# A float32 encoder on one core: seven block products for every round of the channel mixer's second product but the last, and GpSimd for most low parts of the weights

## The chip, the core and the metric

The kernel runs on one core of a Trainium2 chip. The metric is the device time of one execution in microseconds. The engines that matter are TensorE (PE, matmuls; PEld is its weight loads), VectorE (DVE), ScalarE (ACT), GpSimd (POOL) and SyncE (SP, which issues the loads). Each runs its own queue in order; semaphores tie the queues together.

## The reference

The program is a trunk of two residual layers over 256 positions and 2048 channels, in float32.

```python
for i in range(DEPTH):                     # DEPTH = 2
    j = i // 2
    h = rms_norm(x, ...)                   # layer 0: convolution and pooling; layer 1: Fourier mix
    ...
    x = x + mixed @ w_out
    h = rms_norm(x, mlp_norm[i])
    x = x + jnp.square(jax.nn.relu(h @ mlp_w1[i])) @ mlp_w2[i]     # 2048 -> 8192 -> 2048
    g = jax.nn.sigmoid(rms_norm(x, ple_norm[i]) @ ple_w_gate[i])
    x = x + g * (p[i] @ ple_w_proj[i])
return rms_norm(x, final_norm)
```

## The kernel before

**Matmuls in three passes.** A float32 matrix is split into two parts that TensorE takes in its faster float32 form: a high part (hi), and a low part (lo) that is the float minus the high part. A product is hi·hi + hi·lo + lo·hi, three matmuls. Weights are streamed from HBM once, so their splitting runs all the time: `Weights.load` has SP fetch a tile `raw` of 128x2048 floats (1 MB; four buffers), and `Weights.divide` makes `hl` from it (four buffers): ScalarE writes hi (line 112), and another engine writes lo = raw − hi (line 117). Which one is the argument `lo`. Before, that is GpSimd for 28 of the tiles in layer 0's token mixer and VectorE for all others. `next()` hands out one `hl` tile, and calls for the splitting of the three behind it and the loading of two more.

**The channel mixer** (`mlp`) works through the 8192 hidden channels in 16 groups `q` of 512. `w1(q)` makes one group's hidden values in transposed form, with four tiles `hl`: 16 matmuls of 512 columns and 16 of 256 for each; afterwards ScalarE and VectorE evict them (lines 608, 609), apply relu, the norm's scale `rows` and the square, and split them into `h`. Two groups make a round `f`; `w2(f, n)` multiplies them by the 512 output columns number `n` (48 matmuls for each of two tiles).

**Seven block products.** For the output columns 0 and 1 the kernel uses Winograd's form of Strassen's product: the activations of a group are a 2x2 of blocks (128 positions by 256 channels), and so are the weights of two neighbouring column blocks, and seven block products take the place of eight. `pair(f)` does them: per group seven products of two `kt` and three passes each, 42 matmuls, 84 for the two groups. Sums of activation blocks (`form`, split into `g`) come out of `w1`. Sums of weight blocks are made by VectorE in place on the raw tiles (line 109) before they are split: four additions of 128x1024 for each group. Of two pairs of raw tiles seven `hl` tiles come out, two blocks of 128x1024 in each (`SEVEN` is the order of the blocks). Four PSUM results are gathered into `x` and into `sums` (lines 649 to 657), and `pair_end` combines them after the last round.

A round before is thus: `w1(2f+2)`, `w2(f, 2)`, `w2(f, 3)`, `pair(f)`, `w1(2f+3)`.

**Order.** PE and SP run in program order. ACT and DVE are ordered by a scheduler, but for stretches under `in_order()`. `put_off(f, steps)` runs `f` after so many `tick()`s of later matmuls. `embed` is the gated embedding behind the mixer: four products with the gate (`ps_g`) and the small embedding product (`ps_e`) for four column blocks. `rows_product` takes an `hl` tile against activations, with `PASSES_W_MOVES` innermost: for each `kt` and each half of the positions hi·hi, hi·lo, lo·hi.

Of the kernel before, what the change touches and what calls it, by code (L numbers as in the profile page):

```python
# [32 lines left out]
SEVEN = (1, 2, 5, 3, 6, 7, 4), (1, 5, 2, 6, 3, 7, 4)  # L33
RSQRT_MAGIC = float(0x5F3759DF)
# [10 lines left out]
class Weights:  # L45
# [16 lines left out]
    def made(self, steps, lo="vector"):  # L62

        for step in steps:
            for r in (step[1][0], step[2][0]) if step[0] == "add" else (step[1][0],):
                self.last[r] = len(self.todo)
        self.todo.append((steps, lo))

    def add(self, src, cols=2048, pieces=1, lo="vector"):
        r, w = self.source(src, cols, pieces), cols // pieces  # L70
        self.made([("split", (r, i * w), i * w, w) for i in range(pieces)], lo)

    def add_seven(self, tiles):
# [3 lines left out]
        q, parts = 1024, []  # L77
        for k, (x, y) in enumerate(tiles):
# [4 lines left out]
            parts += [(p, *made[p]) for p in SEVEN[k]]  # L83
        for k in range(0, len(parts), 2):
# [4 lines left out]
            self.made(adds + [("split", src, i * q, q) for i, (_, src, _) in two])  # L89
# [12 lines left out]
    def divide(self, after_first=None):  # L102
        n = self.split
        steps, lo = self.todo[n]
        hl = self.hl_pool.tile([P, 2, 2048], F32R, tag="hl", name=f"hl{n}")
        for i, (what, (r, c), other, w) in enumerate(steps):
# [6 lines left out]
            if lo == "dma":  # L113
                self.nc.scalar.activation(hl[:, 1, to], hl[:, 0, to].bitcast(F32), AF.Copy, scale=-1.0)
                self.nc.gpsimd.dma_start(out=hl[:, 1, to], in_=self.srcs[r][0][:, c:c + w], accum_op=ALU.add)
            else:
                getattr(self.nc, lo).tensor_tensor(hl[:, 1, to], src, hl[:, 0, to].bitcast(F32), ALU.subtract)  # L117
# [32 lines left out]
def encoder(ctx: ExitStack, tc: tile.TileContext, a, out: bass.AP):  # L150
# [35 lines left out]
    def add_mlp(i):  # L186
        def w1(q):
            for c in range(4):
                ws.add(a["mlp_w1"][i, q, c], lo="vector")

        def w2(f, n):
            for q in (2 * f, 2 * f + 1):
                ws.add(a["mlp_w2"][i, n, q])

        def pair(f):
            ws.add_seven([(a["mlp_w2"][i, 0, q], a["mlp_w2"][i, 1, q]) for q in (2 * f, 2 * f + 1)])
# [3 lines left out]
        for f in range(8):  # L200
            if f < 7:
                w1(2 * f + 2)
            w2(f, 2)
            if f == 7:
                pair(f)
            w2(f, 3)
            if f < 7:
                pair(f)
                w1(2 * f + 3)

    def add_ple(i):
        for n in range(4):
            parts = [(a["ple_w_gate"][i, n, c], 2048) for c in (2, 0, 1, 3)]
            parts.insert(0 if n == 0 or i == LAYERS - 1 and n == 3 else 4, (a["ple_w_proj"][i, n], 1024))
            for src, cols in parts:
                ws.add(src, cols=cols)
# [33 lines left out]
    rows = const.tile([P, S], F32, name="rows")  # L250
# [43 lines left out]
    class Norm:  # L294
# [35 lines left out]
        def chunk(self, c, steps=4):  # L330
# [7 lines left out]

            self.squares(c)
            put_off(lambda: self.scale(c, turned), steps)  # L340
            if c == 3:
                self.finish()

# [6 lines left out]
    def rows_product(ps, acts, kts, first, last, w=None, ts=(0, 1), cols=slice(0, 512)):  # L350
# [616 lines left out]
```

## Time and profile before

| what | value |
|---|---|
| median of 3 runs | 1976.58 us (1976.06 to 1977.9) |
| profiled execution | 1976.2 us, of which the span of the trace is 1974.4 us |
| PE busy | 1937.8 us, 98% |
| DVE busy | 1567.8 us, 79% |
| ACT busy | 1042.1 us, 53% |
| POOL busy | 128.6 us, 7% |

The span reaches from the program's first instruction to its last; 1.8 us of the profiled execution lie outside it. A busy time is the time in which at least one instruction of the engine was running, waiting inside an instruction included.

### The profile page before, as it was taken

The page shows a single profiled execution, that of the slowest core. Times are in us where ns is not written, and L with a number is a line of the kernel's source. Part 1 is how long each engine was busy: PE and PEld are TensorE (multiplying, and loading weights), DVE is VectorE, ACT ScalarE, POOL GpSimd, SP SyncE. Part 2 cuts the span into 40 slices and gives each one's busy share as a digit, 9 for nine tenths or more (in the row PEclk, how much of TensorE's full clock was granted, in tenths as well). Part 3 has the DMA queues.
Part 4 walks back from the last instruction along what each step waited for, and adds up shares of the span by engine and source line. Part 5 has one row for each costly group of instructions (what it writes and reads, how often), then busy time and mean ns, then how long its engine had stood idle before and what let it go on. Part 6 is the DMA issues. An engine that isn't in the chain of part 4 may idle for free.

```text
span 1974.4 us, 24094 instructions
## 1 busy us (share of the span) xinstructions
PE 1937.8 (98%) x9730; PEld 1649.0 (84%) x9730; DVE 1567.8 (79%) x1771; ACT 1042.1 (53%) x1087; POOL 128.6 (7%) x65
## 2 busy tenths in 40 slices
PE   7999999999999999999999999999999999999897
PEld 6888888888888888887789888888888888888686
DVE  7888868887978889799755556978888797889954
ACT  6445655555555555555555445554555555555543
POOL 2876000000000000000001000000000000000000
PEclk9999999999999999999999999999999999999999
DMA  9556454637456463654543545455463745645542
GB/s 344 182 177 218 171 187 154 235 129 263 177 199 219 154 245 140 244 196 168 188 159 137 199 174 189 171 213 213 150 243 137 260 183 180 235 149 197 224 146 100
DMA packets 55664, 377.43 MB, mean 191 GB/s; under 512 B 6384, under 2 KB 6528, under 8 KB 11648
## 3 DMA queue, kind: packets, MB, share of 16 engines
q1 hardware_dynamic: 55152, 374.82, 52.2%
q8 instruction: 76, 1.25, 0.2%
q10 hardware_dynamic: 144, 1.05, 0.1%
q14 instruction: 36, 0.29, 0.0%
q0 software_dynamic: 256, 0.02, 0.0%
HBM read 373.75 MB, written 2.10 MB: 190 GB/s over the span
## 4 chain that ended last, share of the span: by engine, by line
PE 92%; DVE 5%; issue 1%; ACT 1%; DMA 0%; SPq 0%; ACTq 0%
PE ps_h L593 23%; PE ps_o L358 16%; PE ps_h L598 12%; PE ps_g L358 8%; PE ps_od L358 4%; PE ps_in L358 4%; PE ps_out L358 3%; DVE hl L117 2%; PE ps_pool L358 2%; PE ps_e L358 1%; PE ps_outp L358 1%; DVE raw L109 1%; PE ps_f L371 1%; PE ps_z L802 1%; PE ps_s_6c L672 1%
## 5 line engine op out<-in xcount | busy, mean ns | idle before, releaser
L112 ACT ACTIVATE hl<-raw 128x2048 fp32r<-128x2048 f32 (+2 forms) x529 | 777.1, 1492 | 670.4 <-PE ps_h L598 210.8
L117 DVE TENSOR_TENSOR hl<-raw,hl 128x2048 fp32r<-128x2048 f32 (+3 forms) x501 | 864.8, 1743 | 274.2 <-ACT hl L112 272.6
L593 PE MATMUL ps_h<-xT_mlp,hl 128*128 128x512 f32 x2048 | 488.2, 390 | 0.0
L593 PEld LDWEIGHTS ps_h<-xT_mlp,hl 128*128 128x128 f32 x2048 | 377.3, 188 | 73.7
L358 PE MATMUL ps_o<-hl,h 128*128 128x512 f32 x1536 | 354.0, 391 | 4.6 <-DVE hl L117 4.6
L358 PEld LDWEIGHTS ps_o<-hl,h 128*128 128x128 f32 x1536 | 287.8, 188 | 64.5 <-DVE hl L117 5.5
L598 PEld LDWEIGHTS ps_h<-xT_mlp,hl 128*128 128x128 f32 x2048 | 262.6, 191 | 10.0
L598 PE MATMUL ps_h<-xT_mlp,hl 128*128 128x256 f32 x2048 | 266.0, 283 | 0.0
L358 PE MATMUL ps_g<-hl,xT_ple 128*128 128x512 f32 (+1 forms) x816 | 179.7, 380 | 0.0
L358 PEld LDWEIGHTS ps_g<-hl,xT_ple 128*128 128x128 f32 x816 | 147.2, 190 | 28.5 <-DVE hl L117 0.4
L117 POOL TENSOR_TENSOR hl<-raw,hl 128x2048 fp32r<-128x2048 f32 (+1 forms) x28 | 120.5, 4319 | 57.7 <-ACT hl L112 57.7
L358 PE MATMUL ps_in<-hl,xT_ev 128*128 128x512 f32 x384 | 92.3, 402 | 7.0 <-ACT hl L112 7.0
L455 DVE SCALAR_TENSOR_TENSOR acc<-vp,vT,acc 128x256 f32<-128x256 f32 x240 | 96.4, 481 | 0.1
L358 PEld LDWEIGHTS ps_in<-hl,xT_ev 128*128 128x128 f32 x384 | 74.3, 194 | 23.1 <-ACT hl L112 7.0
L608 ACT ACTIVATE relu<-ps_h 128x512 f32<-128x512 f32 x64 | 38.2, 598 | 97.5 <-PE ps_h L598 97.5
L358 PE MATMUL ps_od<-hl,f 128*128 128x512 f32 x384 | 88.1, 390 | 0.0
L358 PEld LDWEIGHTS ps_od<-hl,f 128*128 128x128 f32 x384 | 71.8, 188 | 14.8
L109 DVE TENSOR_TENSOR raw<-raw 128x1024 f32<-128x1024 f32 x64 | 78.1, 1221 | 1.1
L109 DVE TENSOR_TENSOR raw<-raw,raw 128x1024 f32<-128x1024 f32 x64 | 77.9, 1217 | 0.0
L609 DVE TENSOR_TENSOR relu<-ps_h,relu 128x512 f32<-128x512 f32 x64 | 43.8, 687 | 29.8 <-ACT relu L608 29.8
L816 POOL CAST top<-z 128x4 fp32r<-128x4 f32 x8 | 1.5, 188 | 883.9 <-DVE z L280 883.9
L624 ACT ACTIVATE g<-form 128x512 fp32r<-128x512 f32 x64 | 38.4, 624 | 22.6 <-DVE form L621 11.7
(283 smaller groups left out, 1688.5 us busy)
## 6 DMA issues: line engine op xcount, KB each, us to landing
raw<-in_mlp_w SPq DMA_DIRECT2D x256, 1024.0 KB, 4.9
raw<-in_ple_w_gate SPq DMA_DIRECT2D x32, 1024.0 KB, 5.3
raw<-in_w_in SPq DMA_DIRECT2D x20, 1024.0 KB, 5.0
raw<-in_ev_w_out SPq DMA_DIRECT2D x16, 1024.0 KB, 4.8
raw<-in_od_w_out SPq DMA_DIRECT2D x16, 1024.0 KB, 4.9
raw<-in_w_in SPq DMA_DIRECT2D x16, 256.0 KB, 6.4
raw<-in_ple_w_proj SPq DMA_DIRECT2D x8, 512.0 KB, 3.4
x<-in_x SPq DMA_DIRECT2D x2, 1024.0 KB, 8.6
```

Source lines behind the costliest of these rows:

```text
L109: self.nc.vector.tensor_tensor(src, src, self.raw[other[0]][:, other[1]:other[1] + w], ALU.add)
L112: self.nc.scalar.activation(hl[:, 0, to], src, AF.Copy)
L117: getattr(self.nc, lo).tensor_tensor(hl[:, 1, to], src, hl[:, 0, to].bitcast(F32), ALU.subtract)
L358: nc.tensor.matmul(ps[t][:, cols], lhsT=acts[:, s, kt, t * P:(t + 1) * P], rhs=w[:, m, kt * 512 + cols.start:kt * 512 + cols.stop], start= ...
L371: nc.tensor.matmul(out_ps, lhsT=w[sw], rhs=act[sa], start=bank_first and i == 0, stop=i == n - 1, skip_group_check=True)
L455: nc.vector.scalar_tensor_tensor(acc, src, cwT[:, ch, k:k + 1], acc, ALU.mult, ALU.add)
L593: nc.tensor.matmul(pss[p][:, e], lhsT=w[:, 0, ch], rhs=norm.xT[c][:, :, kt], start=c == 0 and kt == 0, stop=False, skip_group_check=True)
L598: nc.tensor.matmul(pss[p][:, e, 1], lhsT=w[:, 1, ch], rhs=norm.xT[c][:, 0, kt], start=False, stop=c == 3 and kt == 3, skip_group_check=True)
L608: nc.scalar.activation(r, pss[p][:, :, 1], AF.Copy)
L609: nc.vector.tensor_tensor(s, pss[p][:, :, 0], r, ALU.add)
L624: nc.scalar.activation(g[:, 0, to], src, AF.Copy)
L672: nc.tensor.matmul(psum(p), lhsT=act, rhs=w[:, j, col:col + 512], start=q % 2 == 0 and kt == 0 and m == 0, stop=q % 2 == 1 and kt == 1 and ...
```

## The change

1. `w2(f, n)` goes, but for the last round. `pair(f, n)` does the seven block products for the columns 0, 1 (`n` = 0) and for 2, 3 (`n` = 2). A round is now `w1(2f+2)`, `pair(f, 0)`, `w1(2f+3)`, `pair(f, 2)`. The second set of sums lies in `more` and `most`. In the last round the columns 2, 3 are done by eight products as before.
2. The low parts: in `w1` three of four tiles by GpSimd (all of `w1(0)` and the tile c = 3 of the others stay with VectorE), in `pair` the blocks of the list `aside` by GpSimd (6 of 14), the w2 tiles of the last round, the first half of the gate's tiles for two column blocks, and the first embedding product's weights too. VectorE keeps the sums of weight blocks and the other low parts.
3. ACT and DVE run in program order through all rounds. What follows the eviction of `w1` (relu, square, the sums of blocks, the splits) is now `rest()`, put off to behind the first matmuls of the next `w1` or `w2`.
4. `rows_product` first does hi·hi and lo·hi for all `kt` of both halves and then all products with the weights' low part, so that it needs lo late and all four `kt` of the activations early.
5. The end of the mixer and the start of the gate are reordered (the norm's transposes are put off behind `pair(7, 0)` and the first gate tiles; the gate starts with the two column blocks 0, 1 against channels c = 2, 3). `diag` is made by ACT.

```diff
-        self.todo.append((steps, lo))
+        self.todo.append(steps)
...
-    def add_seven(self, tiles):
+    def add_seven(self, tiles, aside):
...
+            parts += [("gpsimd" if p in aside[k] else "vector", *made[p]) for p in SEVEN[k]]
...
+            made_of.append(adds + [("split", src, i * q, q, lo) for i, (lo, src, _) in two])
+        for steps, later in zip(made_of, made_of[1:]):
+            if steps[0][0] == later[0][0] == "add" and later[0][1] != steps[-1][1]:
+                steps.insert(-1, later.pop(0))
...
+            getattr(self.nc, lo[0]).tensor_tensor(hl[:, 1, to], src, hl[:, 0, to].bitcast(F32), ALU.subtract)
...
-                ws.add(a["mlp_w1"][i, q, c], lo="vector")
+                ws.add(a["mlp_w1"][i, q, c], lo="vector" if q == 0 or c == 3 else "gpsimd")
...
+        def pair(f, n):
+            ws.add_seven([(a["mlp_w2"][i, n, q], a["mlp_w2"][i, n + 1, q]) for q in (2 * f, 2 * f + 1)],
+                         ((1, 2, 3, 7), (1, 2) if f < 7 else (1, 2, 3, 7)))
...
+        steps = [(t, kt, sm) for sms in (((0, 0), (1, 0)), ((0, 1),)) for t in ts for kt in kts for sm in sms]
...
+            ss = [work.tile([P, 2, S], F32, name="relu2", tag="sv") for p in range(2)]
+            for p, s in enumerate(ss):
+                r = work.tile([P, 2, S], F32, name="half", tag="sr")
                 with tc.high_priority(offset=PRIO):
                     nc.scalar.activation(r, pss[p][:, :, 1], AF.Copy)
                     nc.vector.tensor_tensor(s, pss[p][:, :, 0], r, ALU.add)
+            def rest():
...
-        for f in range(8):
-            if f < 7:
-                w1(2 * f + 2)
-            w2(f, 2)
-            if f < 7:
-                w2(f, 3)
-                with in_order():
-                    pair(f)
-                w1(2 * f + 3)
...
+        with in_order():
+            for f in range(7):
+                rest = w1(2 * f + 2)
+                pair(f, 0)
+                put_off(rest, 1)
+                rest = w1(2 * f + 3)
+                pair(f, 2)
+                put_off(rest, 1)
+            put_off(lambda: pair_end(2), 2)
+            pss = {n: psum_mm(f"ps_o{i}_{n}") for n in (2, 3)}
+            for q in (14, 15):
+                for n in (2, 3):
+                    rows_product(pss[n], hidden[q], range(4), q == 14, q == 15)
...
+            pair(7, 0)
```

**GpSimd's queue.** Before, it splits up to `hl33` in layer 0's token mixer, and then does small work of the Fourier mix in layer 1:

```order
L117 TENSOR_TENSOR hl31_1424<-raw31_1357,hl31_1424 128x2048
L117 TENSOR_TENSOR hl32_1464<-raw32_1393,hl32_1464 128x2048
L117 TENSOR_TENSOR hl33_1493<-raw33_1422,hl33_1493 128x2048
L791 MEMSET top_7902 128x512
L816 COPY top_7902<-z0_7948 128x2x2 x2
```

Now its queue runs on through the rounds. These are the rows of `pair(2, 2)` of layer 0 (`hl111` to `hl117`; its blocks come from `raw96` to `raw99`) and of the `w1` behind it (`hl118` to `hl121`, of which `hl121` is not here):

```order
L121 TENSOR_TENSOR hl111_4142<-raw96_4062,hl111_4142 128x1024 x2
L121 TENSOR_TENSOR hl112_4181<-raw97_4083,hl112_4181 128x1024
L121 TENSOR_TENSOR hl113_4222<-raw97_4083,hl113_4222 128x1024
L121 TENSOR_TENSOR hl114_4268<-raw98_4179,hl114_4268 128x1024
L121 TENSOR_TENSOR hl115_4289<-raw98_4179,hl115_4289 128x1024
L121 TENSOR_TENSOR hl118_4351<-raw100_4306,hl118_4351 128x2048
L121 TENSOR_TENSOR hl119_4368<-raw101_4328,hl119_4368 128x2048
L121 TENSOR_TENSOR hl120_4387<-raw102_4349,hl120_4387 128x2048
```

So in every half round (one `w1`, one `pair`) six operations of 128x1024 and three of 128x2048 stand where none stood.

**VectorE's queue.** Before, at the start of the seven blocks of `pair(2)` in layer 0 (`raw92` to `raw95`):

```order
L109 TENSOR_TENSOR raw92_3838<-raw92_3838,raw93_3904 128x1024
L625 TENSOR_TENSOR g0_6_3892<-form1_3894,g0_6_3892 128x512
L379 TENSOR_TENSOR x_81<-ps_o0_2_2_3903,x_81 128x512 x2
L117 TENSOR_TENSOR hl99_3967<-raw93_3904,hl99_3967 128x1024
L117 TENSOR_TENSOR hl99_3967<-raw92_3838,hl99_3967 128x1024
L109 TENSOR_TENSOR raw93_3904<-raw93_3904 128x1024
L109 TENSOR_TENSOR raw92_3838<-raw92_3838,raw93_3904 128x1024
L117 TENSOR_TENSOR hl100_3999<-raw93_3904,hl100_3999 128x1024
```

Now, from the last block before `pair(2, 2)` starts on PE to the last but two of it:

```order
L121 TENSOR_TENSOR hl113_4222<-raw96_4062,hl113_4222 128x1024
L634 TENSOR_TENSOR relu2_4260<-ps_h0_70_4081,half_4262 128x512
L634 TENSOR_TENSOR relu2_4261<-ps_h0_71_4082,half_4265 128x512
L117 TENSOR_TENSOR raw96_4062<-raw96_4062 128x1024
L117 TENSOR_TENSOR raw98_4179<-raw98_4179,raw99_4188 128x1024
L121 TENSOR_TENSOR hl114_4268<-raw96_4062,hl114_4268 128x1024
L121 TENSOR_TENSOR hl115_4289<-raw98_4179,hl115_4289 128x1024
L117 TENSOR_TENSOR raw99_4188<-raw99_4188 128x1024
L117 TENSOR_TENSOR raw98_4179<-raw98_4179,raw99_4188 128x1024
L121 TENSOR_TENSOR hl116_4308<-raw99_4188,hl116_4308 128x1024
L121 TENSOR_TENSOR hl116_4308<-raw98_4179,hl116_4308 128x1024
L117 TENSOR_TENSOR raw98_4179<-raw98_4179 128x1024
```

And behind the gathers of `pair(2, 2)`, where `hl121` is the fourth tile of the next `w1` and `raw104` the first of the next `pair`:

```order
L121 TENSOR_TENSOR hl121_4409<-raw103_4366,hl121_4409 128x2048
L640 SCALAR_TENSOR_TENSOR relu_4421<-relu2_4260,rows0_2095 128x512
L640 SCALAR_TENSOR_TENSOR relu_4424<-relu2_4261,rows0_2095 128x512
L650 TENSOR_TENSOR form1_4429<-relu2_4260 128x256
L651 TENSOR_TENSOR form0_4428<-relu2_4261,relu2_4260 128x256
L652 TENSOR_TENSOR form0_4428<-relu2_4260,form0_4428 128x256
L653 TENSOR_TENSOR form1_4429<-relu2_4261,form0_4428 128x256
L657 TENSOR_TENSOR h0_7_4420<-relu2_4260,h0_7_4420 128x2x128
L657 TENSOR_TENSOR h0_7_4420<-relu2_4261,h0_7_4420 128x512
L660 TENSOR_TENSOR g0_7_4427<-form0_4428,g0_7_4427 128x512
L660 TENSOR_TENSOR g0_7_4427<-form1_4429,g0_7_4427 128x512
L117 TENSOR_TENSOR raw104_4385<-raw104_4385,raw105_4407 128x1024
```

The evictions (L634) now stand in the middle of the weights' sums and splits, and `rest()` stands behind the split of `hl121`. All of these operations but L634 and the gathers read two operands from SBUF; those two read one from PSUM. Per half round VectorE has eight sums and eight splits of 128x1024, one split of 128x2048, the two L640, four `form`, two splits of `h` (one of half width) and two of `g`, two L634 and the gathers.

## Rows read from the trace of the kernel before

**Rows 1.** The page: span, and busy time, share and instructions of each engine.

```profile
span 1974.4 us, 24094 instructions
...
PE 1937.8 (98%) x9730; PEld 1649.0 (84%) x9730; DVE 1567.8 (79%) x1771; ACT 1042.1 (53%) x1087; POOL 128.6 (7%) x65
```

**Rows 2.** Windows: one round, and the start (us, PE, PEld, DVE, ACT, POOL, clock, DMA, GB/s).

```profile
406.66:491.99 85.33, 85.33 (x438) 73.15 (x437) 72.09 (x67) 45.72 (x42) 0.00 (x0) 1.00 0.53 197
...
12.00:18.00 6.00, 6.00 (x28) 4.90 (x28) 5.95 (x12) 6.00 (x14) 0.00 (x0) 1.00 1.04 400
```

**Rows 3.** Timeline of PE in that round (start us, us, what, how many).

```profile
406.66 21.95 PE L358 MATMUL ps_o<-hl,h 128*128 128x512 f32 x96
428.45 1.52 PE L672 MATMUL ps_s_1a<-hl,h 128*128 128x512 f32 x6
```

**Rows 4.** DVE in that round by shape (busy us, mean ns | idle before, releaser).

```profile
L117 DVE TENSOR_TENSOR hl<-raw,hl 128x2048 fp32r<-128x2048 f32 x12 | 27.2, 2288 | 10.5 <-ACT hl L112 10.4
L117 DVE TENSOR_TENSOR hl<-raw,hl 128x1024 fp32r<-128x1024 f32 x14 | 16.8, 1219 | 0.1
...
L610 DVE SCALAR_TENSOR_TENSOR relu<-relu,rows 128x512 f32<-128x512 f32 x4 | 2.8, 692 | 0.1
...
L620 DVE TENSOR_TENSOR form<-relu,form 128x256 f32<-128x256 f32 x2 | 0.8, 420 | 0.0
```

**Rows 5.** ACT in that round by shape.

```profile
L112 ACT ACTIVATE hl<-raw 128x2048 fp32r<-128x2048 f32 x12 | 22.9, 1915 | 17.7 <-PE ps_h L598 13.8 <-DMA raw<-in_mlp_w 1.9 <-PE ps_s_1d L672 1.4
L112 ACT ACTIVATE hl<-raw 128x1024 fp32r<-128x1024 f32 x14 | 14.3, 1056 | 14.3 <-DVE raw L109 8.8 <-PE ps_o L358 4.7 <-PE ps_s_1b L672 0.8
```

**Rows 6.** Timeline of DVE in that round's pair: the first and last of eleven.

```profile
432.12 1.22 DVE L109 TENSOR_TENSOR raw<-raw,raw 128x1024 f32<-128x1024 f32 x1
...
443.86 1.22 DVE L657 TENSOR_TENSOR sums<-ps_s_1a,sums 128x1024 f32<-128x1024 f32 x1
```

**Rows 7.** POOL by shape, 31 to 181 us.

```profile
L117 POOL TENSOR_TENSOR hl<-raw,hl 128x2048 fp32r<-128x2048 f32 x24 | 111.0, 4635 | 55.7 <-ACT hl L112 55.7
L117 POOL TENSOR_TENSOR hl<-raw,hl 128x1024 fp32r<-128x1024 f32 x4 | 9.7, 2417 | 2.0 <-ACT hl L112 2.0
```

**Rows 8.** Timeline of POOL, 28 to 182 us.

```profile
31.27 9.53 POOL L117 TENSOR_TENSOR hl<-raw,hl 128x2048 fp32r<-128x2048 f32 x2 [29.59 <-ACT hl L112]
...
157.15 22.98 POOL L117 TENSOR_TENSOR hl<-raw,hl 128x2048 fp32r<-128x2048 f32 x5 [1.10 <-ACT hl L112]
```

**Rows 9.** Timeline of DVE, 27 to 182 us.

```profile
27.30 4.48 DVE L117 TENSOR_TENSOR hl<-raw,hl 128x2048 fp32r<-128x2048 f32 x2
...
33.21 3.05 DVE L286 TENSOR_SCALAR rstd_ev<-rs_m 128x2 int32<-128x2 int32 x1
36.29 4.53 DVE L287 TENSOR_SCALAR rstd_ev<-rstd_ev 128x2 int32<-128x2 int32 x1
...
160.84 0.48 DVE L280 SCALAR_TENSOR_TENSOR y_pool<-ps_pw,vT,y_pool 128x256 fp32r<-128x256 f32 x1 [0.27 <-ACT y_pool L275]
...
178.93 3.35 DVE L117 TENSOR_TENSOR hl<-raw,hl 128x2048 fp32r<-128x2048 f32 x1 [0.71 <-ACT hl L112]
```

**Rows 10.** DVE by shape, 120 to 300 us: two groups with an operand in PSUM.

```profile
L280 DVE SCALAR_TENSOR_TENSOR xT_mlp<-tr_mlp,vT,xT_mlp 128x256 fp32r<-128x256 f32 x16 | 7.0, 478 | 0.6 <-ACT xT_mlp L275 0.6
...
L280 DVE SCALAR_TENSOR_TENSOR y_pool<-ps_pw,vT,y_pool 128x256 fp32r<-128x256 f32 x8 | 3.8, 481 | 1.4 <-ACT y_pool L275 1.3
```

**Rows 11.** Who waited for whom: PE (us in total, times, longest).

```profile
PE ps_o L358 <- DVE hl L117: 4.6, 2, 2.3
...
PE tr_ple L336 <- DVE xT_ple L280: 2.8, 2, 1.7
PE tr_ple L336 <- DVE rs_m L285: 2.6, 2, 1.3
PE tr_ple L336 <- DVE x L651: 2.1, 2, 1.8
```

**Rows 12.** The page: DMA issues (KB each, us from issue to landing).

```profile
raw<-in_mlp_w SPq DMA_DIRECT2D x256, 1024.0 KB, 4.9
```

**Rows 13.** Timelines at the start (ACT) and at layer 0's pooled product (PE).

```profile
8.39 1.88 ACT L112 ACTIVATE hl<-raw 128x512 fp32r<-128x512 f32 x3 [0.54 <-DMA raw<-in_w_in]
...
157.48 5.63 PE L358 MATMUL ps_out<-hl,y_pool 128*128 128x512 f32 x24
```

More of the change, by code (lines that the diff above doesn't have):

```diff
@@ L60, in source, with made @@
         return len(self.srcs) - 1
-    def made(self, steps, lo="vector"):
+    def made(self, steps):
         for step in steps:
@@ L66, in made @@
                 self.last[r] = len(self.todo)
[L67 removed]
+        self.todo.append(steps)
     def add(self, src, cols=2048, pieces=1, lo="vector"):
         r, w = self.source(src, cols, pieces), cols // pieces
[L71 to L77 removed]
+        self.made([("split", (r, i * w), i * w, w, lo) for i in range(pieces)])
+    def add_seven(self, tiles, aside):
+        q, parts, made_of = 1024, [], []
         for k, (x, y) in enumerate(tiles):
@@ L88, in add_seven @@
             two.sort(key=lambda part: (len(part[1][2]) > 0, part[0]))
-            self.made(adds + [("split", src, i * q, q) for i, (_, src, _) in two])
+            made_of.append(adds + [("split", src, i * q, q, lo) for i, (lo, src, _) in two])
+        for steps, later in zip(made_of, made_of[1:]):
+            if steps[0][0] == later[0][0] == "add" and later[0][1] != steps[-1][1]:
+                steps.insert(-1, later.pop(0))
+        for steps in made_of:
+            self.made(steps)
     def load(self, after_first=None):
@@ L103, in divide @@
         n = self.split
-        steps, lo = self.todo[n]
+        steps = self.todo[n]
         hl = self.hl_pool.tile([P, 2, 2048], F32R, tag="hl", name=f"hl{n}")
-        for i, (what, (r, c), other, w) in enumerate(steps):
+        for i, (what, (r, c), other, w, *lo) in enumerate(steps):
             src = self.raw[r][:, c:c + w]
@@ L337, in turned, with chunk @@
                 return tr
+            self.scale(c, turned, (h,))
+        def chunk(self, c, steps=(4, 4), finish=None):
             self.squares(c)
-            put_off(lambda: self.scale(c, turned), steps)
-            if c == 3:
+            for h in range(2):
+                put_off(lambda h=h: self.turn(c, h), steps[h])
+            if c == 3 and finish is None:
                 self.finish()
+            elif finish:
+                put_off(self.finish, finish)
     def psum_mm(name):
@@ L570, in mlp @@
         hidden, forms = {}, {}
+        rows = small.tile([P, S], F32, name=f"rows{i}", tag="ln_rs", bufs=1)
+        more = work.tile([P, 1024], F32, name=f"sums15_{i}", tag="once", bufs=1)
+        most = [work.tile([P, 512], F32, name=f"sums{k}_{i}", tag="vp") for k in (7, 6)]
+        totals = {0: {5: [sums[:, :1024]], 7: [sums[:, 1024:]]}, 2: {5: [more], 7: most}}
         def scales():
@@ L637, in pair @@
+            return rest
+        def pair(f, n):
             tiles = {}
+            cols = n * 512
             def psum(p):
```

286 lines of the change are left out of this document (149 added, 137 removed).

## The prediction

> **What bounds the kernel now.** I read the page's busy times first [rows 1]: PE 98%, VectorE 79%, GpSimd 7%. PE is the bound, and the next question is where. The windows give one round of the mixer as 85.33 us in which PE is busy all the time, VectorE 72.09, ScalarE 45.72 and GpSimd 0 [rows 2]; seven rounds a layer, 14 in all, are 1194.6 of the 1974.4 us. PE's timeline divides a round [rows 3]: `w2` for columns 2 and 3 runs from 406.66 to 428.45, 21.79 us for 96 matmuls, 0.227 each; the 84 of `pair` at that rate are 19.07; what is left of 85.33, 44.47, are two `w1` of 22.24. The view of waits shows what PE waits for elsewhere: at the two layer ends [rows 11], 12.1 us in its four longest groups there. The profiled execution took 1976.2 us (1.8 outside the span), 0.4 under the median; the sum is made against 1976.2.
>
> **The change, part by part.**
>
> *Matmuls.* In 14 rounds 84 matmuls take the place of 96: 12 x 0.227 = 2.72 us a round, 38 us. A half round (`w1` and `pair`) would be 22.24 + 19.07 = 41.31 us of PE, if all its weights came in time.
>
> *What the weights cost in a half round.* VectorE has eight sums and eight splits of 128x1024. Such instructions, one behind the other, start 1.17 us apart: ten steps from 432.12 to 443.86 [rows 6], so 16 x 1.17 = 18.7. The split of 128x2048 is 2.29 [rows 4], 2.2 when another follows. `rest()` is two L640 (0.69, so 1.3), four `form` (0.42, so 1.7), and splits of `h` and `g` worth 0.42 + 3 x 0.66 = 2.4: 5.4. Together 26.3. Two evictions (1.3) and the gathers (4.5) come on top: 32 us of 41.31. GpSimd has six times 2.417 and three times 4.635 [rows 7]: 28.4. ScalarE has 14 x 1.06, 4 x 1.92 [rows 5] and some 4.5: 27. Each engine for itself fits under PE. So the question is whether VectorE and GpSimd can work at the same time.
>
> *They did not, where the trace shows it.* GpSimd works in a row from 157.15 to 180.13 [rows 8]. VectorE's split of 128x2048 that starts at 178.93 takes 3.35 us [rows 9] where the same instruction takes 2.29 [rows 4]: 1.06 more, and 1.20 of GpSimd's run were left. The other way round: GpSimd's two operations from 31.27 take 9.53, where five take 22.98, so 9.2 for two [rows 8]; VectorE's split ran to 31.78 [rows 9], 0.51 into the first. And the two small integer instructions of 33.21 and 36.29 take 3.05 and 4.53 us and end, at 36.26 and 40.82, with GpSimd's two operations. With an operand in PSUM nothing is held: 481 ns while GpSimd works (`y_pool`), 478 while it rests (`xT_mlp`) [rows 10]. That is also how before lives with GpSimd in layer 0: there VectorE mostly reads PSUM.
>
> The Trainium skill says it as a rule (SBUF — State Buffer, "Who interferes with whom"): a VectorE instruction with two inputs in SBUF and a GpSimd instruction that reads SBUF exclude each other for the whole instruction, and one with at most one SBUF input does not contend. This case's trace agrees in the rows named: 3.35 for 2.29 us, 481 for 478 ns. By the rule the half round has the sum below for its floor; without it, PE's 41.31.
>
> *The floor of a half round.* All 26.3 us above read two operands from SBUF; the evictions and gathers read PSUM and go free. So the two engines share one resource for 26.3 + 28.4 = 54.7 us: 13.4 more than PE needs.
>
> *The loop.* It is a little longer, since the queues do not always have work for the port. I lay one half round out, from e = 0, where VectorE ends `hl113` (names as in the rows of the order). I let a held instruction go first when the holder ends, as at 36.24, and GpSimd go next when it was waiting behind VectorE. The evictions end at 1.3. ScalarE makes `hl114`'s first block by 1.1; GpSimd splits it till 3.5; VectorE's sum on `raw96`, held since 1.3, runs to 4.7, the sum on `raw98` to 5.9, the split of `hl114` to 7.05. Meanwhile ScalarE made `hl115` ready; GpSimd takes the port till 9.45. Eight VectorE instructions follow, to 18.8. The last two free the raw tiles of the next `w1`'s third and fourth weights, at 17.6 and 18.8. A load takes 4.9 us [rows 12]; for one behind another I add 2.6, a megabyte at 400 GB/s [rows 2]: 22.5 and 25.0. ScalarE is through with the fourth at 26.9. GpSimd, which could not begin the first before 19.5, is then in its second till 28.7; VectorE splits the fourth till 30.9, GpSimd the third till 35.5, and only then `rest()` starts, held by it. Its chain of ScalarE and VectorE steps is 4.1 us, so that ScalarE comes to `hl122` at 39.6 and has it at 40.6. GpSimd's two splits last till 45.4. From here they alternate: sum to 46.6, GpSimd 49.0, sum 50.2, split 51.4, GpSimd 53.8, sum 55.0, ScalarE 56.1, split 57.3, which is e again. **The half round takes 57.3 us**, floor 54.7. PE waits for the second block of every `pair`, since its PSUM tile is freed by the eviction behind that last split.
>
> *The sum.* In a layer, from the end of `w1(1)`: the first e comes at about 30 (`w1(2)` 22.2 and 8 for the port's backlog: some 58 us of work on it in the 44.5 of two `w1`); 13 steps of 57.3 are 744.9; from the last e to the end of its `pair` some 20. That is 795, where before has 7 x 85.33 = 597.3: +198 a layer, +396. `pair(7, 0)`: from its fourth tile on five sums and four splits of VectorE and four of GpSimd, 20.2 us on the port, where PE allows about 15: +5 a layer, +10. The layer ends: the transposes are put off behind `pair(7, 0)` and gate tiles, so the waits of [rows 11] go: −12. `rows_product` needs all four `kt` of the activations in its first seven matmuls. At the start the second to fourth quarter of the first weights come from 9.02 to 10.27 [rows 13], and two matmuls a quarter do not bridge that: some +1.2. At `ps_out` the last quarter of `y_pool` is there at 161.32 [rows 9], and is now wanted at 157.48 + 7 x 0.227 = 159.1 [rows 13]: +2.2. Late low parts of weights are worth nothing here, since PE does not wait for them in the rounds. 1976.2 + 396 + 10 − 12 + 3 = **2373 us**.
>
> *Bounds.* With the floor of 54.7 the 26 steps give 68 less; without backlog and without the 10, another 26: 2279. If GpSimd wins the contests that I gave to VectorE (the split of `hl121` and the first sum), one operation of 2.4 to 4.6 comes into the loop; with 2.9 on each step it is 2448.
>
> **The rivals.**
>
> *No exclusion: faster.* If splits by GpSimd and VectorE's two-operand instructions run side by side, only the loop of loads and splits counts. With the same steps and no holds it is: from the sum on `raw98` 11.7 us to the last split, 6.2 to the landing, 1.9 + 2.2 for the fourth tile's parts, 4.1 for `rest()`, 1.06 + 2.42 for `hl122`'s first block, 4 x 1.17 for sum, sum, split and sum, 1.06 for the last sum's block, 1.2 for ScalarE's evictions, 1.06 + 2.42 for the next block: 40.0, just under PE's 41.31. Then 1976.2 − 38 − 12 + 3 = 1929 us. It is decided where a two-operand VectorE instruction starts inside a GpSimd operation: at its usual length this rival holds, and each microsecond by which it is longer in the loop costs, beyond the 1.3 of slack, 26 to 28 us in total. For it speaks that each engine alone fits; against it stand both directions in [rows 8, 9].
>
> *Sharing in part: slower, but less.* If only part of an instruction excluded (half of the 26.3, say), the loop would lie between 41.3 and 54.7: 1990 to 2270. Against it: 1.06 of the 1.20 us left were waited for.
>
> *More than the loop.* If every contest goes against the instruction that is in the loop, or the scheduler's queues block ScalarE too, each step is over 60 us: above 2450.
>
> **How the numbers follow.** Exclusion with the loop as laid out, 54.7 to 60 us a step: 0.77. Sharing in part: 0.10. More: 0.05. No exclusion: 0.08, of which 0.07 ends faster and 0.01 within 0.2%, which is about what a measurement of this kernel can tell from no change (4 us). The first case is the forecast, 2373 us, with its own bounds, 2279 to 2448. The range adds a few us above for the two layer ends, and below the upper quarter of the sharing in part, to 2200, with 0.03 of its chance: 2200 to 2455 holds 0.80. Faster 0.07, same 0.01, slower 0.92.
>
> **What would show each step.** Port: VectorE's splits and sums of 128x1024 (now 1.22) have means well above 1.5 us in the rounds, GpSimd's of 128x1024 above 2.42; evictions stay at 0.69. Loop: half rounds of 55 to 60 us, PE's largest wait at the second block of `pair` for the eviction, PE's share under 85%. Matmuls: 168 fewer. Layer ends: no `tr_ple` waits. Start: PE's first tile some 1 us later, `ps_out` 2. The prediction is wrong if the 128x1024 splits keep 1.22 us beside a busy GpSimd, or if a half round is near 41 us.

## The result, and the profile after

The changed kernel takes 2336.46 us (median; 2336.23 to 2337.13), the kernel before 1976.32: 1.182 times as long (95% interval 1.180 to 1.184). The forecast was 2373 and the range 2200 to 2455. The page's first lines, against [rows 1]:

```profile
span 2335.3 us, 24560 instructions
...
PE 1986.8 (85%) x9562; PEld 1668.2 (71%) x9562; DVE 1806.9 (77%) x1749; ACT 1126.5 (48%) x1237; POOL 1187.8 (51%) x359
```

There are 168 fewer matmuls, and yet PE is busy longer: part of them run at a lower clock. No engine is near its full time. Two half rounds by windows (columns as in [rows 2]), from the second block of one `pair` to that of the next, and the start of one:

```profile
379.24:432.97 53.73, 44.35 (x213) 37.38 (x213) 41.41 (x32) 27.57 (x29) 32.43 (x10) 0.88 0.43 157
432.97:486.73 53.76, 43.19 (x213) 36.55 (x213) 43.48 (x34) 25.69 (x26) 32.45 (x10) 0.91 0.42 156
...
379.24:386.00 6.76, 6.76 (x18) 5.33 (x19) 6.09 (x5) 2.95 (x3) 3.56 (x2) 0.56 0.44 151
```

A half round is 53.7 us where PE needs 41.31. VectorE and GpSimd are busy for 43.48 + 32.45 = 75.9 of 53.76 us, and much of that is waiting inside instructions, as VectorE's groups over the whole run show (mean ns of one; before, such instructions of 128x1024 took 1219 [rows 4]):

```profile
L121 DVE TENSOR_TENSOR hl<-raw,hl 128x1024 fp32r<-128x1024 f32 x242 | 364.8, 1509 | 65.3 <-ACT hl L120 65.3
L117 DVE TENSOR_TENSOR raw<-raw 128x1024 f32<-128x1024 f32 x120 | 236.1, 1968 | 2.1
...
L117 DVE TENSOR_TENSOR raw<-raw,raw 128x1024 f32<-128x1024 f32 x120 | 215.9, 1799 | 67.4 <-POOL hl L121 66.4
L640 DVE SCALAR_TENSOR_TENSOR relu<-relu,rows 128x512 f32<-128x512 f32 x64 | 164.4, 2602 | 0.3
...
L634 DVE TENSOR_TENSOR relu<-ps_h,half 128x512 f32<-128x512 f32 x64 | 41.2, 677 | 43.5 <-ACT half L633 43.5
```

Of these groups all with two operands in SBUF are stretched; L634, which reads PSUM, is not. Not every instruction with two operands in SBUF is hit: L652 and L653 (`form`, 128x256) keep 424 ns (420 before [rows 4]), since they fall where GpSimd waits for ScalarE (in the half round below from 466.05 to 471.00). GpSimd's splits have means of 2.77 and 5.05 us where they took 2.417 and 4.635 [rows 7]. In one half round (timelines of GpSimd, then VectorE, then PE; start us, us):

```profile
419.85 5.69 POOL L121 TENSOR_TENSOR hl<-raw,hl 128x1024 fp32r<-128x1024 f32 x2
...
437.74 2.50 POOL L121 TENSOR_TENSOR hl<-raw,hl 128x1024 fp32r<-128x1024 f32 x1 [3.20 <-ACT hl L120]
450.18 15.87 POOL L121 TENSOR_TENSOR hl<-raw,hl 128x2048 fp32r<-128x2048 f32 x3 [9.95 <-ACT hl L120]
```

```profile
423.36 3.26 DVE L117 TENSOR_TENSOR raw<-raw 128x1024 f32<-128x1024 f32 x1
...
432.24 1.27 DVE L634 TENSOR_TENSOR relu<-ps_h,half 128x512 f32<-128x512 f32 x2
...
436.75 1.23 DVE L121 TENSOR_TENSOR hl<-raw,hl 128x1024 fp32r<-128x1024 f32 x1
...
449.47 1.22 DVE L694 TENSOR_TENSOR sums<-ps_s_10a,sums 128x1024 f32<-128x1024 f32 x1
...
459.28 2.29 DVE L121 TENSOR_TENSOR hl<-raw,hl 128x2048 fp32r<-128x2048 f32 x1 [5.73 <-ACT hl L120]
461.49 5.71 DVE L640 SCALAR_TENSOR_TENSOR relu<-relu,rows 128x512 f32<-128x512 f32 x2
```

```profile
422.04 1.55 PE L707 MATMUL ps_s_10a<-hl,h 128*128 128x512 f32 x6
432.97 2.93 PE L707 MATMUL ps_s_10b<-hl,h 128*128 128x512 f32 x6 [9.38 <-DVE relu L634]
```

The sum at 423.36 starts inside GpSimd's two splits, which end at 425.54, and ends 1.08 us behind them, at 426.62. The three gathers from 449.47 to 452.95 read PSUM and run at their usual 1.21 us beside GpSimd's first split of 128x2048. The split at 459.28 takes its usual 2.29, and it is GpSimd that waits: its three take 15.87 us for 13.9 [rows 7]. Then the first of the two L640 waits for GpSimd's third, and the pair takes 5.71 for 1.38 us [rows 4]. PE's wait comes earlier: from 423.59 to 432.97, 9.38 us, it waits for the eviction (L634 at 432.24), which stands in VectorE's queue behind the held sums and splits.

Where the 360.9 us of the span went, by the starts and ends in PE's timeline (rounds: from the first matmul of `w1(0)` to the first of the last round; last round and gate: from there to the end of the last gate matmul):

| stretch | before | after | more |
|---|---|---|---|
| up to the first `w1` | 253.3 | 254.8 | 1.5 |
| seven rounds, layer 0 | 643.1 | 790.2 | 147.1 |
| last round and gate, layer 0 | 152.8 | 187.1 | 34.3 |
| Fourier mixer | 117.1 | 117.7 | 0.6 |
| seven rounds, layer 1 | 643.1 | 788.9 | 145.7 |
| last round and gate, layer 1 | 154.8 | 186.6 | 31.8 |

### The profile page after: what moved, and what is told of

It reads as the page before. It is cut to its first block, busy times and chain, and to the rows that moved or that the text cites. A ratio compares the mean times of both kernels' runs of the same rounds, so it can differ in the third digit from the quotient of the medians.

```text
span 2335.3 us, 24560 instructions
## 1 busy us (share of the span) xinstructions
PE 1986.8 (85%) x9562; PEld 1668.2 (71%) x9562; DVE 1806.9 (77%) x1749; ACT 1126.5 (48%) x1237; POOL 1187.8 (51%) x359
## 4 chain that ended last, share of the span: by engine, by line
DVE 42%; PE 20%; ACT 11%; DMA 8%; issue 8%; POOL 3%; ACTq 0%; DVEq 0%; SPq 0%; POOLq 0%
DVE hl L121 17%; DVE raw L117 13%; ACT hl L120 8%; DMA raw<-in_mlp_w 8%; PE ps_g L379 7%; DVE relu L640 6%; PE ps_od L379 3%; POOL hl L121 3%; PE ps_out L379 3%; PE ps_h L620 3%; ACT relu L641 1%; PE ps_h L625 1%; DVE x L720 1%; DVE relu L634 1%; PE ps_outp L379 1%
## 5 line engine op out<-in xcount | busy, mean ns | idle before, releaser
L121 POOL TENSOR_TENSOR hl<-raw,hl 128x1024 fp32r<-128x1024 f32 (+1 forms) x320 | 1176.6, 3695 | 898.4 <-ACT hl L120 898.4
L120 ACT ACTIVATE hl<-raw 128x1024 fp32r<-128x1024 f32 (+2 forms) x669 | 865.3, 1326 | 803.6 <-DVE raw L117 488.0
L121 DVE TENSOR_TENSOR hl<-raw,hl 128x1024 fp32r<-128x1024 f32 (+3 forms) x349 | 596.4, 1714 | 282.5 <-ACT hl L120 282.5
L625 PEld LDWEIGHTS ps_h<-xT_mlp,hl 128*128 128x128 f32 x2048 | 262.3, 191 | 10.4 <-POOL hl L121 0.8
L117 DVE TENSOR_TENSOR raw<-raw,raw 128x1024 f32<-128x1024 f32 x120 | 215.9, 1799 | 67.4 <-POOL hl L121 66.4
L117 DVE TENSOR_TENSOR raw<-raw 128x1024 f32<-128x1024 f32 x120 | 236.1, 1968 | 2.1
L640 DVE SCALAR_TENSOR_TENSOR relu<-relu,rows 128x512 f32<-128x512 f32 x64 | 164.4, 2602 | 0.3
L641 ACT ACTIVATE relu<-relu 128x512 f32<-128x512 f32 x64 | 39.5, 631 | 203.6 <-DVE relu L640 203.4
L634 DVE TENSOR_TENSOR relu<-ps_h,half 128x512 f32<-128x512 f32 x64 | 41.2, 677 | 43.5 <-ACT half L633 43.5
L379 PE MATMUL ps_o<-hl,h 128*128 128x512 f32 x192 | 49.6, 422 | 14.3 <-DVE h L657 14.3
L379 PEld LDWEIGHTS ps_o<-hl,h 128*128 128x128 f32 x192 | 39.6, 207 | 24.0 <-DVE h L657 15.2
```

What stands on the lines that cost most here:

```text
L117: self.nc.vector.tensor_tensor(src, src, self.raw[other[0]][:, other[1]:other[1] + w], ALU.add)
L120: self.nc.scalar.activation(hl[:, 0, to], src, AF.Copy)
L121: getattr(self.nc, lo[0]).tensor_tensor(hl[:, 1, to], src, hl[:, 0, to].bitcast(F32), ALU.subtract)
L379: nc.tensor.matmul(ps[t][:, cols], lhsT=acts[:, s, kt, t * P:(t + 1) * P], rhs=w[:, m, kt * 512 + cols.start:kt * 512 + cols.stop], start= ...
L625: nc.tensor.matmul(pss[p][:, e, 1], lhsT=w[:, 1, ch], rhs=norm.xT[c][:, 0, kt], start=False, stop=c == 3 and kt == 3, skip_group_check=True)
L634: nc.vector.tensor_tensor(s, pss[p][:, :, 0], r, ALU.add)
```

## The experiments

**What the hold is made of.** First GpSimd's share was given back to VectorE, and then its reading was taken away.

```diff
-                ws.add(a["mlp_w1"][i, q, c], lo="vector" if q == 0 or c == 3 else "gpsimd")
+                ws.add(a["mlp_w1"][i, q, c], lo="vector")
...
-                         ((1, 2, 3, 7), (1, 2) if f < 7 else (1, 2, 3, 7)))
+                         ((), ()))
```

> The changed kernel, but in all rounds of the mixer VectorE makes every low part; GpSimd has nothing to do there. Exclusion (VectorE's two-operand instructions and GpSimd's splits wait for each other): the sums and splits of 128x1024 fall back from 1.5 to 2.0 us to about 1.22, and a half round is VectorE's own work: 22 x 1.17 for sums and splits of 128x1024, 4 x 2.2 for w1, 5.4 for rest(), 1.3 evictions, 4.5 gathers = 45.7 us, against 53.74 now and 41.31 of PE. 26 half rounds: 2336 - 26 x 8 = 2128, at 47 us a half round 2161; so 2115 to 2165. Rival (VectorE is slowed by something else: the loads, ScalarE, a clock): the means stay at 1.8 to 2.0 us, VectorE's queue gets longer still, and the time is above 2336. Rival (the length comes from the order of the queues alone): half rounds stay near 53 us although nothing is held.

2135.94 us, 1.081 (1.080 to 1.083). Over the run:

```profile
L121 DVE TENSOR_TENSOR hl<-raw,hl 128x1024 fp32r<-128x1024 f32 x426 | 511.3, 1220 | 13.1 <-ACT hl L120 13.1
...
L117 DVE TENSOR_TENSOR raw<-raw,raw 128x1024 f32<-128x1024 f32 x120 | 146.6, 1221 | 2.0
```

The means are back at 1.22 us, and 200 us with them, although VectorE now does all splits itself: the stretching comes from GpSimd. A half round is 47.86 us; VectorE is busy for 44.82 of it. What sets its length is not VectorE's work alone. At the start of nearly every `w1` PE waits for the gather that frees its PSUM, and the 16 matmuls behind the wait are slower (3.82 us is their usual time):

```profile
480.31 6.28 PE L620 MATMUL ps_h<-xT_mlp,hl 128*128 128x512 f32 x16 [3.88 <-DVE sums L694]
```

41.31 + 3.88 + 2.46 is 47.65 us. The run with eight products below has the same wait, and the run behind it ends it with two lines.

```diff
+            if lo[0] == "zero":
+                for _ in range(2):
+                    self.nc.gpsimd.memset(hl[:, 1, to].bitcast(F32), 0.0)
+                continue
             getattr(self.nc, lo[0]).tensor_tensor(hl[:, 1, to], src, hl[:, 0, to].bitcast(F32), ALU.subtract)
```

> The changed kernel, but where GpSimd would subtract in the mixer's w1 and pair it fills the low part with zeros twice over (two fills, which read nothing and do not wait for ScalarE's high part; the low parts of those weights are left out of the product). GpSimd stays busy for a similar time. Theory 1 (it is GpSimd's reading of SBUF that excludes VectorE's two-operand instructions): VectorE's sums of 128x1024 are back at 1.22 us beside a busy GpSimd, the half round is PE's 41.31 us, and the time is 2336 - 26 x 12.4 = 2013 or less, down to some 1960 with the layer ends and the last pair relieved too. Rival 2 (any work of GpSimd on SBUF excludes it, writes too): the means stay at 1.8 to 2.0 us, the half round at 50 us or more, the time near 2300. Rival 3 (the loop is long by its waits, not by the holds): the half round stays above 45 us while the means are 1.22.

1970.65 us, 0.9975 (0.9965 to 0.9984). One half round by windows, and VectorE over the run:

```profile
405.54:446.85 41.31, 41.31 (x214) 35.46 (x213) 31.95 (x34) 25.83 (x26) 22.08 (x18) 1.00 0.53 203
```

```profile
L117 DVE TENSOR_TENSOR raw<-raw 128x1024 f32<-128x1024 f32 x120 | 146.5, 1221 | 2.1
```

GpSimd is busy for 22.08 us writing the same places, VectorE's means are 1.22 us, and the half round is PE's 41.31 to the hundredth. If writing excluded too, 22.1 + 26.3 = 48.4 us would have been the floor. So it is the reading. The fills also don't wait for ScalarE, which the subtraction did; that freedom alone cannot explain the means.

The Trainium skill (SBUF — State Buffer, "Who interferes with whom") says it in so many words: two SBUF inputs on VectorE contend "with a GpSimd instruction that reads SBUF, not with one that only writes it". Both halves of the sentence are borne out here, 1.97 against 1.22 us. The prediction's shorter form, that an instruction with at most one SBUF input does not contend, is too wide: the Trainium skill says this in the same section only of instructions outside VectorE's 2-port performance modes, and in [rows 9] two integer instructions with one SBUF input (lines 286 and 287) were held for 3.05 and 4.53 us; the same two take 0.17 us each where GpSimd rests (at 1146.99 and 1147.19 in the changed kernel). No run shows which mode they were in.

**When does it cost time?** In the kernel before, GpSimd took over splits step by step: one w1 tile of four; three of four (`c < 3`); these and three of the seven tiles of `pair`.

```diff
-                ws.add(a["mlp_w1"][i, q, c], lo="vector")
+                ws.add(a["mlp_w1"][i, q, c], lo="gpsimd" if q > 1 and c == 1 else "vector")
```

> The kernel before, but the second of the four w1 tiles of the groups 2 to 15 has its low part made by GpSimd: two operations of 128x2048 a round. Exclusion: per round the two engines share one resource for VectorE's 72.09 less some 10 us that read PSUM, less 2 x 2.2, plus 2 x 4.635 = 67 us, well under PE's 85.33. Some VectorE instructions show up to 4.6 us more, but PE does not wait: 1976 us, 1972 to 1982. Rival (a hold costs wherever it falls, since the splits are only three tiles ahead): 14 rounds x 2 holds x up to 4.6 us, up to 2105, some 2000 to 2040 likely. No exclusion: 1976 and no VectorE instruction longer than before.

1975.35 us, 0.9999 (0.9991 to 1.0008).

> The kernel before, but GpSimd makes the low part of three of the four w1 tiles of the groups 2 to 15: six operations of 128x2048 a round. If the sum on the shared port decides: VectorE's two-operand work of a round before is 72.09 less what reads PSUM (gathers 4.2, additions to x 2.7, evictions 2.7), 62.4 us; less 6 x 2.29, plus 6 x 4.635 makes 76.5 us, under PE's 85.33: the rounds stay at 85.33 and the time at 1976, or 2 to 5 us a round more where holds fall together in the two w1 that stand side by side, up to 2040. If holds cost whenever they occur, each of the 84 operations up to 4.6 us: some 2100 to 2300. Without exclusion 1976.

1978.59 us, 1.0018 (1.0009 to 1.0027). One round by windows and VectorE's L610 in it:

```profile
406.60:491.90 85.30, 85.30 (x437) 73.13 (x436) 62.44 (x61) 45.81 (x43) 29.59 (x6) 1.00 0.55 198
```

```profile
L610 DVE SCALAR_TENSOR_TENSOR relu<-relu,rows 128x512 f32<-128x512 f32 x4 | 6.5, 1613 | 0.1
```

VectorE is held (1.613 for 0.692 us), and PE does not notice it in the rounds: seven of them take 643.1 us in each layer, as before.

```diff
-            self.made(adds + [("split", src, i * q, q) for i, (_, src, _) in two])
+            self.made(adds + [("split", src, i * q, q) for i, (_, src, _) in two], "gpsimd" if k in (0, 4, 8) else "vector")
```

> The same, and GpSimd also makes the low parts of three of the seven tiles of every pair (six blocks of 128x1024 a round): on the port 76.5 - 6 x 1.22 + 6 x 2.417 = 83.7 us a round, 98% of PE's 85.33. By the port's sum this is the edge: the pair's stretch, 19.07 us of PE against some 33 of the port, is more than three tiles ahead can bridge, so I expect rounds of 87 to 91 us and 2000 to 2060. If only the sum over the round counts, 1976. Without exclusion VectorE is relieved by 21 us a round and the time is 1976 too.

2078.75 us, 1.052 (1.051 to 1.054), more than was expected (2000 to 2060). A round is 91.20 us; two of PE's four waits in a `pair`:

```profile
441.52 3.00 PE L672 MATMUL ps_s_1c<-hl,g 128*128 128x512 f32 x12 [1.10 <-DVE x L379]
...
450.57 1.43 PE L672 MATMUL ps_s_1a<-hl,g 128*128 128x512 f32 x5 [1.65 <-POOL hl L117]
```

So the price of GpSimd's splits rises with the sum on the shared resource, as the expectations add it up: nothing to be seen at 67 of 85.33 us a round, at most 0.3% at 76.5, 5% at 83.7, where it falls short inside `pair` before the round is full, and 18% with 54.7 of 41.31 in the changed kernel's half round (of its 361 us, 293 lie in the rounds).

**The rest of the change.** Eight products for the columns 2 and 3 again, VectorE for the splits of the rounds, all else kept:

```diff
-                pair(f, 2)
+                for n in (2, 3):
+                    ps = psum_mm(f"ps_o{i}_{f}_{n}")
+                    for q in (2 * f, 2 * f + 1):
+                        rows_product(ps, hidden[q], range(4), q == 2 * f, q == 2 * f + 1)
+                    add_to_x(ps, n)
```

> All of the change but its two main parts: columns 2 and 3 are done by eight block products again (a round is w1, pair for columns 0 and 1, w1, then the 96 matmuls for columns 2 and 3), and VectorE makes the low parts in w1 and pair. Kept are program order, rest(), the order of rows_product, the layer ends, and GpSimd for the last round's w2 tiles and half of the gate's. If program order and the putting off cost nothing, a round is 85.33 us as before, and the layer ends decide: as the prediction had them, -12 + 3, so 1967; as the changed kernel's trace has them (PE still waits some 10 us for the transposes), 1974 to 1980. If program order is itself part of the loss, rounds are longer than 85.33, each us 14 us in total: above 1985.

2082.01 us, 1.054 (1.052 to 1.055): the last case by its number, but not by its reason. PE and VectorE behind a `pair`:

```profile
525.64 6.46 PE L622 MATMUL ps_h<-xT_mlp,hl 128*128 128x512 f32 x16 [3.88 <-DVE sums L696]
```

```profile
519.87 4.49 DVE L121 TENSOR_TENSOR hl<-raw,hl 128x2048 fp32r<-128x2048 f32 x2 [0.57 <-ACT hl L120]
524.28 1.22 DVE L696 TENSOR_TENSOR sums<-ps_s_20a,sums 128x1024 f32<-128x1024 f32 x1
```

The gather that frees PSUM for `w1` stands behind two splits for that `w1`. The kernel before has two lines in `pair` (`ws.hold`) that hold those splits back until the first gather is issued; the change takes them out. Put back:

```diff
+            hold, ws.hold = ws.hold, min(ws.hold, ws.used + 7)
...
+                        ws.hold = hold
```

> The kernel with eight block products (2082.0 us), and put back into it what the change took out of pair(): while a pair's matmuls are issued, the splitting of the tiles behind it is held until its first gather has been issued. There PE waited in every round 3.88 us for the gather that stood in VectorE's queue behind two splits of 128x2048, and its next 16 matmuls took 6.4 for 3.8 us at the lower clock. If that is the whole loss of the rounds, 14 x 6.5 = 91 us go: 1991, 1984 to 1997, with the layer ends as they are. If program order or the putting off of rest() costs by itself, PE waits in the rounds elsewhere and the time stays above 2000.

1997.20 us, 1.011 (1.010 to 1.013): 85 us for two lines (1984 to 1997 was expected), and a round (407.50 to 492.83) is 85.33 us as before. Program order and `rest()` cost the rounds nothing. In the changed kernel itself the missing lines should cost nothing either: there GpSimd splits three of those four tiles, and PE's list of waits has none at the start of a `w1`. No run put the lines back there with all else kept.

```diff
-                ws.add(a["mlp_w2"][i, n, q], lo="gpsimd")
+                ws.add(a["mlp_w2"][i, n, q])
...
-        for cs, lo in (((2, 3), "gpsimd"), ((0, 1), "vector")):
+        for cs, lo in (((2, 3), "vector"), ((0, 1), "vector")):
```

> The same with the splitting held, and VectorE makes the low parts of the last round's w2 tiles and of the gate's and the first embedding product's weights as well: GpSimd has no low parts left behind layer 0's token mixer. So it is the kernel before in other orders. In the run with eight products two subtractions of the mixer's end took 3.62 and 4.98 us for 0.69 beside GpSimd's gate tiles, and PE waited 2.2 + 8.0 us a layer for the transposes behind them. If the exclusion makes the layer ends slow, that goes: 20 us less than the kernel with the hold alone, more with the clock, and the prediction's -12 + 3 for the orders may come out: 1964 to 1974. If the new order itself is what is slow, the waits for the transposes stay at 8 us or more and the time at 1985 or more.

1989.20 us, 1.0074 (1.0061 to 1.0086). The 8.0 us less than with the hold alone, where 20 were expected, are GpSimd's holds at the layer ends. 14 us over the kernel before remain, the expectation's second case by the time: in its profile 4.2 and 7.3 from the first `w1` to the last gate matmul of each layer, and 4.0 ahead of that (0.8 in the run before it, which is the same there). So the new order of the layer ends is not better than the old one. PE's waits in layer 0's last round and gate (engine, what, releaser: us in total, times, longest), in the changed kernel, then here:

```profile
PE tr_ple L351 <- DVE x L720: 6.9, 2, 6.0
PE ps_o L379 <- DVE h L657: 6.6, 1, 6.6
PE ps_s_70d L707 <- DVE hl L121: 5.6, 2, 4.8
PE ps_s_70b L707 <- DVE x L401: 4.7, 1, 4.7
PE tr_ple L351 <- DVE xT_ple L294: 3.5, 1, 3.5
```

```profile
PE tr_ple L353 <- DVE x L687: 4.5, 1, 4.5
PE tr_ple L353 <- DVE xT_ple L296: 1.6, 1, 1.6
PE ps_s_70d L710 <- DVE hl L121: 1.4, 1, 1.4
```

Here PE still waits 6.1 us for the transposes of this layer and 8.0 for those of layer 1; before, the three groups of [rows 11] were 7.5 for both layers together. One small part of the new orders was tried alone in the kernel before, the loop of `rows_product` as the change has it (its `steps` line):

> The kernel before with one small part of the change: rows_product does hi times hi and lo times hi for all first, and the products with the weights' low part last. The prediction gave it 1.2 us at the start and 2.2 at ps_out, 3.4 together: 1979. The layer ends it had at -12 by another part. In the changed kernel the mixer's first matmul is 1.5 us later than before, so 1977.5 by that. If the order is what makes the layer ends and the last round of the mixer slow (a wait for the activations' last channels), there are waits before ps_o, ps_g or ps_e that the kernel before does not have, and up to 14 us more, the 1989 of the kernel with the hold and no GpSimd.

1975.97 us, 1.0003 (0.9994 to 1.0012). In its trace the first `w1` starts 1.9 us later and the two last stretches are 1.1 and 1.3 shorter. So the order of `rows_product` is not what makes them longer.

**Better balances.** All seven-product rounds, the hold put back, and one w1 tile of four by GpSimd (`lo="gpsimd" if q > 1 and c == 1`, and `((), ())` for the blocks of `pair`):

> All seven-product rounds of the changed kernel, with the splitting held in pair(), and GpSimd making the low part of one w1 tile a half round instead of three and six blocks of pair. By the exclusion VectorE then has 45.7 - 2.2 = 43.5 us a half round, the shared port 26.3 + 6 x 1.17 + 3 x 2.2 - 2.2 ... that is 39.9 - 2.2 + 4.6 = 42.3, PE 41.31: half rounds of 43.5 to 45 us, 2135.9 - 26 x (47.84 - 43.5) = 2023, up to 2062. Without exclusion 43.5 too, so this tells only how far the balance carries: no split of the work between the two engines brings VectorE and the port below PE at once. If the hold costs a wait of its own, half rounds stay at 47 us.

2140.98 us, 1.084 (1.082 to 1.085): half rounds of 44.6 to 50.1 us, so no gain appears beside VectorE alone (2135.94 us). Two things differ between these runs, the tile and the hold, and no run has VectorE alone with the hold; what the tile by itself costs is therefore not shown. In one half round of 47.36 us VectorE is busy for 45.74: the split that it lost (2.2) comes back as a hold, 5.52 us for a split of 2.28.

```profile
669.22 6.62 POOL L121 TENSOR_TENSOR hl<-raw,hl 128x2048 fp32r<-128x2048 f32 x1 [40.74 <-DVE x L682]
```

```profile
672.48 5.52 DVE L121 TENSOR_TENSOR hl<-raw,hl 128x2048 fp32r<-128x2048 f32 x1 [1.11 <-ACT hl L120]
```

The other way was the kernel before with seven products for all columns in three rounds of each layer:

```diff
+            if f in (1, 3, 5):
+                with in_order():
+                    pair(f, 2)
+                w1(2 * f + 3)
+                with in_order():
+                    pair(f, 0)
+                continue
             w2(f, 2)
```

> The kernel before, but the rounds 1, 3 and 5 of each layer are w1, pair for columns 2 and 3, w1, pair for columns 0 and 1 (seven products for all columns), with one w1 tile of each group there split by GpSimd; the other rounds and the layer ends are as before. Such a round has 2 x 43.5 us for VectorE and 82.6 for PE, the others 72 and 85.33: if the tiles split ahead carry over the difference of 4.4 us, the gain is the matmuls alone, 6 x 2.72 = 16.3 us: 1960. If nothing carries over, each such round costs 2 x 2.2 us: 6 x 4.4 = 26 more, 1986. If it goes wrong in one place, PE shows a wait there six times.

2018.41 us, 1.022 (1.020 to 1.023). Such a round takes 90.69 us, VectorE busy for 86.42 of them, near the 2 x 43.5 laid out for it: nothing is carried over from the rounds that leave VectorE time. Another 4.3 us are lost beyond VectorE's work, and so the time lies above both cases of the expectation; PE's single waits in these `pair` are 0.5 to 2.2 us long. No version here that computes the low parts beats the kernel before.

## Why the prediction was right

**The exclusion** was right in direction, place and kind: the means, PE's wait at the second block of `pair` for the eviction, PE at 85%, gathers and evictions at their usual length. The runs with VectorE alone and with a GpSimd that only writes show it as the cause. Two of the signs came out weaker: the sums have means of 1.97 and 1.80 us, but the splits 1.51, not well above 1.5, and the half rounds lie below the 55 to 60 us.

**The loop** was mis-sized: 57.3 us a half round were laid out, 53.74 measured, below the stated floor of 54.7. The floor summed instructions at full length, but where the work passes from one engine to the other the second ends sooner behind the first than that. GpSimd's split at 437.74 ends 2.26 us behind VectorE's of 436.75 for the 2.417 used, VectorE's held sum ends 1.08 us behind GpSimd's splits (426.62 and 425.54) for the 1.17 used, and GpSimd's five in [rows 8] took 22.98, 4.60 each for 4.635. By an estimate from the ends of all these instructions between 432.97 and 486.73 that is some 2.0 of the 3.6 us. The rest is that the layout left the port unused for 2.6 us a half round, waiting for ScalarE, while in this stretch neither engine uses it for 1.0 us in all, the longest time from 449.56 to 450.18: a queue on either side nearly always had something ready. That is 13 x 3.6 = 46 us a layer; the rest of the difference lies in the way into the loop and out of it. Over the two layers' rounds +293 us were measured; +396 were forecast.

**The layer ends** are the step that failed: "the transposes are put off behind `pair(7, 0)` and gate tiles, so the waits of [rows 11] go: −12", with +10 for `pair(7, 0)`. Measured are +34.3 and +31.8. The small sums of the mixer's end, 0.69 us each, come between GpSimd's gate tiles, each of which holds them once (VectorE's timeline; GpSimd splits gate tiles from 1115.68 on without a break):

```profile
1125.12 4.86 DVE L720 TENSOR_TENSOR x<-x,sums 128x512 f32<-128x512 f32 x1
1129.90 4.98 DVE L720 TENSOR_TENSOR sums<-sums 128x512 f32<-128x512 f32 x1
```

More is lost before that, in the last round itself. There `rest()` of the last group stands beside GpSimd's four splits for the w2 tiles (19.34 us from 1041.62 on), and two `form` of 0.42 us are held:

```profile
1051.77 4.83 DVE L650 TENSOR_TENSOR form<-relu 128x256 f32<-128x256 f32 x1
1056.53 4.71 DVE L651 TENSOR_TENSOR form<-relu,relu 128x256 f32<-128x256 f32 x1
```

Behind them PE waits 6.6 us for `h` in the last round's product. In `pair(7, 0)` it waits 11.6 us in all, where the prediction put +5 a layer; the transposes account for 10.4 us of the waits listed above (6.9 and 3.5).

The prediction counted the port only in the rounds and in `pair(7, 0)`, and here priced a moved wait as a removed one. Without GpSimd the layers are still 4.2 and 7.3 us longer than before; `rows_product` is excluded as the cause, and which of the other moves it is stays open. By itself, then, the reordering costs some 11 us where −12 stood.

**The two errors partly cancel**: 103 us too much in the rounds, some 68 too little at the ends. The forecast was 37 us off; that it came closer than its parts is luck.

**Start**: 3.4 forecast, 1.5 measured, 1.9 with the order of `rows_product` alone; the waits are where they were put (0.96 us at the second quarter, 0.92 at `ps_out`).

**Passed over**: the two lines of `ws.hold`. PE does not wait where they would act here, but with VectorE splitting for `w1` they were worth 85 us in the run with eight products, and the run with VectorE alone pays the same wait in every half round.

**The rival "no exclusion"** gave 1929 us. The run whose GpSimd does not read comes to 1970.65 with the half rounds at 41.31 as that rival had them. What is missing to it is again the layer ends: 167.7 and 169.9 us, 14.9 and 15.1 more than before, where GpSimd still subtracts for the last round's w2 tiles and the gate. The rival of sharing in part is answered by the 1.08 us: of a held instruction of 1.22 us little more than a tenth overlaps with its holder.

## What to carry to other kernels

Before work is moved from VectorE to GpSimd, add up for each stretch, not for the whole run, VectorE's instructions with two SBUF operands and GpSimd's that read SBUF, as if one engine did them. If the sum stayed well under the bounding engine, the move was free here (67 of 85.33 us) or nearly so (76.5); if not, a split that took 1.22 us on VectorE costs 2.4 of the same resource on GpSimd. Here no division helps: by an estimate from the prediction's terms VectorE's 45.7 us and the port's 39.9 meet at some 43 when between one and two w1 tiles of a half round move, and eight products need only 42.67 (half of 85.33).

When part of a change is taken out, see which of its other parts leaned on it: lines that look idle in one version (the hold) carry 85 us in another.

## What was not expected of the hardware

PE's granted clock fell after a wait as short as 3.88 us. In the run with eight products it was 0.57 in the 6.46 us behind that wait (the third value from the end):

```profile
525.64:532.10 6.46, 6.46 (x18) 5.13 (x19) 6.46 (x5) 1.91 (x1) 0.00 (x0) 0.57 0.96 377
```

The 16 matmuls of 512 columns took 6.46 us there for 3.82, so some 6.5 us a round were lost for a wait of 3.88. After the 11.5 us wait of the changed kernel the granted clock was 0.56 in the following 6.76 us (between its levels of 1.2 and 2.4 GHz, mostly the lower), and the first six matmuls took 2.93 us for 1.52. There it should cost little, since the port and not PE sets the half round; no run shows it apart.
